# Fused matmul, GELU, matmul on one core: W1 sums of tiles 0 and 1 made in the head, sums of x(1) spread over four periods, W1 stores spread, the last output store issued by ScalarE

## The chip, the cores and the metric

One core of one Trainium2 chip. The metric is the device time of one execution in microseconds (us). The kernel before took 853.16 us in the median of six runs (853.0 to 853.53).

## The reference

```python
batch, m, k, h, n = 16, 512, 768, 3072, 768
def reference(x, w1, b1, w2):          # float32 in, float32 out
    y = np.matmul(x, w1) + b1
    y = 0.5 * y * (1.0 + erf(y / np.sqrt(2.0)))
    return np.matmul(y, w2).astype(np.float32)
```

## The kernel before

Both products are done with a seven-product scheme on 2x2 blocks: each output tile needs seven products of sums of blocks instead of eight products of blocks. The sums are made by VectorE in float16 (line L191, the helper `tt`). The 8192 rows are taken in eight groups of 1024; the argument is about the first two, x(0) and x(1), which share each W1 tile while it is in the on-chip memory. Cuts are marked with `# ...`.

W1 tile n arrives raw (four blocks); four sums complete it. The tile is later stored whole, to be read back for the other row groups:

```python
def keep(n):
    nc.sync.dma_start(out=w1s[hi_of(n)][:], in_=wts[n])

def prep_wt(n):
    o = {s: w1_op(wts[n], s) for s in range(7)}
    for d, a, b in ((T3, B22, T1), (T1, T1, B11), (T2, B22, T1), (T4, B21, T2)):
        later(KQ * P, lambda d=d, a=a, b=b: tt(o[d], o[a], o[b], SUB), soon)
```

TensorE works in periods. A period holds products p1, p5, p6, p2 of unit i and p7, p3, p4 of the unit before it, j; after each, `fill(slot)` puts other work into the queues:

```python
def copy_xy(u):                       # ScalarE; L604
    # ...
    nc.scalar.copy(out=bY[u.g % 2][:, 0:u.F], in_=bX[u.g % 2][:, 0:u.F])

def p7(u):
    u.mm(7, bY[u.g % 2], False, 0, u.C)
    add_c22(u)                        # VectorE; L611: reads bY
    # ...

def p6(u):
    u.mm(6, bY[u.g % 2], False, 0, u.C)
    # ... for the first row groups:
    nc.vector.tensor_copy(out=bZ[:, 0:u.F], in_=bY[u.g % 2][:, 0:u.F])   # L657

def period(i, j, fill):
    # ... (other kinds of units)
    p1(i, 0, i.C)
    copy_xy(i)
    p7(j)
    fill(1)
    p5(i)
    fill(2)
    p3(j)                             # VectorE add of bZ; L639
    fill(3)
    p6(i)
    j.right_done()                    # ScalarE GELU on what L611 and L639 made; L402
    fill(4)
    p4(j)                             # ScalarE GELU; L407
    fill(5)
    p2(i)                             # ScalarE GELU; L407
    fill(6)
```

Each engine takes its queue in order, so an instruction that waits holds up all behind it (in the timeline below VectorE stands 0.55 us at a load, and the add L639, which does not need it, comes after the sums that do). And p7 of a unit adds onto bY, so it can't start before L657 has read bY, while p6 needs bY filled by L604.

The first 24 periods are filled by `fill_a`. Period 7 is `at[1, 0]`, the first that uses x(1). The loads of the early phase are all issued at its start, W1 tile 6 last:

```python
def loads_a(pos):
    if pos == 0:
        load_wt(4)
        load_next_x(1, (0, 4, 1, 5))
        load_wt(5)
        load_next_x(1, (2, 6, 3, 7))
        load_wt(6)
    # ...

X1_PE = (3, 7)

def fill_a(pos, slot):
    # ...
    if pos == at[1, 0] - 2 and slot in (2, 5):
        transpose_pe(1, X1_PE[slot // 3])          # TensorE transposes, then a ScalarE copy
    if slot == (1 if pos < at[1, 0] else 4) and pos + 1 < len(seq) and seq[pos + 1][0] == 0:
        prep_wt(seq[pos + 1][1])                   # in period 5: W1 tile 6
    if slot == 4:
        if pos in (3, 6):
            prep_wt(pos // 6)                      # W1 tiles 0 and 1
        # ...
    if slot == 1:
        if pos in (at[1, 0] - 2, at[1, 0] - 1):
            h = pos - at[1, 0] + 2
            x_sums(1, soon, slice(h * RH // 2, (h + 1) * RH // 2))
        # ...
```

The last product of the last unit ends with two half sums, each stored at once:

```python
def last(self, banks):
    for t in range(2):
        self.mm(4, banks[t], True, 0, self.C, (t,))
        o = self.dst[:, 1, t, 0, :]
        tt(o, banks[t][:, t * N4:(t + 1) * N4], o, ADD)
        nc.sync.dma_start(out=orr[:, self.sb * 8 + 2 + t, N2:N2 + N4], in_=o)
```

Of the kernel before, what the change touches and what calls it, by code (L numbers as in the profile page):

```python
# [10 lines left out]
P = 128  # L11
ADD = mybir.AluOpType.add
SUB = mybir.AluOpType.subtract
# [4 lines left out]
B11, B21, T1, B22, T3, T2, T4 = range(7)  # L18
# [4 lines left out]
def kernel(  # L23
# [8 lines left out]
    nc = tc.nc  # L32
# [5 lines left out]
    RH = SB // 2  # L38
    nsb = R // SB
    KQ = K // P // 2  # L40
    NH = H // P // 2
    N2 = N // 2
# [3 lines left out]
    orr = out.rearrange("b (s p) n -> p (b s) n", p=P)  # L46
# [4 lines left out]
    N4 = N2 // 2  # L51
# [69 lines left out]
    def w1_op(wt, slot):  # L121
        raw = wt[:, 0:4 * KQ * P].rearrange("p (a k b c) -> p a b k c", a=2, k=KQ, b=2)
        if slot in RAW:
            return raw[:, RAW[slot][0], RAW[slot][1]]
        return wt[:, slot * KQ * P:(slot + 1) * KQ * P].rearrange("p (k c) -> p k c", c=P)
# [60 lines left out]
    with tc.manual_schedule():  # L186

        soon, queue, late, slow = [], [], [], []

        def tt(o, a, b, op):  # L190
            nc.vector.tensor_tensor(out=o, in0=a, in1=b, op=op)  # L191

        def later(n, f, q=None):
            (queue if q is None else q).append((70 + n * 0.52, f))

        def sums(ns):

            for q in (soon, queue):
                while q and ns >= q[0][0] * 0.6:
                    ns -= q[0][0]  # L200
                    q.pop(0)[1]()

        def flush(q):
            while q:
                q.pop(0)[1]()
# [18 lines left out]
        def keep(n):  # L224
            nc.sync.dma_start(out=w1s[hi_of(n)][:], in_=wts[n])

        def prep_wt(n):
            o = {s: w1_op(wts[n], s) for s in range(7)}
            for d, a, b in ((T3, B22, T1), (T1, T1, B11), (T2, B22, T1), (T4, B21, T2)):
                later(KQ * P, lambda d=d, a=a, b=b: tt(o[d], o[a], o[b], SUB), soon)  # L230

        def load_w2(k, c0, c1):
            nc.gpsimd.dma_start(out=w2rows[k][:, c0:c1, :], in_=w2r[:, k, c0:c1, :])
# [3 lines left out]
        def prep_w2(d, c, q):  # L237
            a, b = {T1: (T3, B11), T2: (B22, T1), T3: (B22, T3), T4: (B21, T2)}[d]
            o = [w2v[s][:, :, c:c + W2C, :] for s in (d, a, b)]
            later(2 * W2C * N4, lambda: tt(*o, SUB), q)  # L240
# [58 lines left out]
        def xT_of(sb, t):  # L299
            return XTs[sb][:, t // NU, :, (t % NU) * P:(t % NU + 1) * P]  # L300

        def transpose_dma(sb, t):
            nc.sync.dma_start_transpose(out=xT_of(sb, t), in_=xhs[t])
# [5 lines left out]
        def transpose_pe(sb, t, copy=nc.scalar.copy):  # L309
            for kc in range(2 * KQ):  # L310
                nc.tensor.transpose(out=bT[t % 2][:, kc, :], in_=xhs[t][:, kc * P:(kc + 1) * P],
                                    identity=ident[:])
            copy(out=xT_of(sb, t), in_=bT[t % 2][:])

        def blocks(sb):
            XT = XTs[sb]
            return [XT[:, a, c:c + KQ, :] for a in range(2) for c in (0, KQ)]

        def x_sums(sb, q, r=slice(0, RH), ks=range(4)):
            A11, A12, A21, A22 = [a[:, :, r] for a in blocks(sb)]  # L320
            S1, S2, S4 = [a[:, :, r] for a in XSs[sb]]
            n = KQ * len(range(RH)[r])
            ops = ((S1, A21, A22, ADD), (S2, S1, A11, SUB), (A21, A11, A21, SUB), (S4, A12, S2, SUB))
            for k in ks:
                later(n, lambda k=k: tt(*ops[k]), q)

        def g_sum(k, U, c0=0, c1=NH, q=None):
            G1, G2 = g_of(U // NU)
            r = slice(U % NU * P, (U % NU + 1) * P)
            g11, g21 = G1[:, c0:c1, 0, r], G1[:, c0:c1, 1, r]  # L330
            g12, g22 = G2[:, c0:c1, 0, r], G2[:, c0:c1, 1, r]
            s = [t[:, c0:c1, :] for t in GS]
            a, b, op = ((g21, g22, ADD), (s[0], g11, SUB), (g11, g21, SUB), (g12, s[1], SUB))[k]
            later((c1 - c0) * P, lambda: tt(s[k], a, b, op), q)
# [128 lines left out]
        class Unit3:  # L463
# [33 lines left out]
            def last(self, banks):  # L497
                for t in range(2):
                    self.mm(4, banks[t], True, 0, self.C, (t,))
                    o = self.dst[:, 1, t, 0, :]  # L500
                    tt(o, banks[t][:, t * N4:(t + 1) * N4], o, ADD)
                    nc.sync.dma_start(out=orr[:, self.sb * 8 + 2 + t, N2:N2 + N4], in_=o)

            def quarter(self, o, r, h):
                return o[:, r, :, h, :]
# [251 lines left out]
        def plain(n, row, side, half, r=slice(0, RH)):  # L757
            slot = ((B11, T1), (B21, B22))[half][side]
            for c in range(KQ):
                nc.tensor.matmul(out=banks[n, row][side][:, r], lhsT=w1_op(wts[n], slot)[:, c, :],  # L760
                                 rhs=blocks(0)[2 * row + half][:, c, r],
                                 start=half == 0 and c == 0 and r.start == 0,
                                 stop=half == 1 and c == KQ - 1, skip_group_check=True)

        def plain_done(n, row, side):
            nc.scalar.activation(out=Gs[0][side][:, n, row, :], in_=banks[n, row][side][:, 0:RH],
                                 func=GELU, bias=b1t[:, 2 * n + side:2 * n + side + 1])

        top, bottom = slice(0, 2 * P), slice(2 * P, RH)
        for half in range(2):  # L770
            for side in range(2):
                plain(0, 0, side, half)
        for side in range(2):
            plain_done(0, 0, side)
        plain(1, 0, 0, 0)
        transpose_pe(0, 4)
        plain(1, 0, 0, 1)
# [23 lines left out]
        plain_done(1, 1, 0)  # L801
        plain(1, 1, 1, 0, bottom)
        prep_wt(2)
        last = [soon.pop()]
        for k in (2, 3):
            for r in (top, bottom):
# [5 lines left out]
        seq = ([(0, k) for k in range(7)] +  # L812
               [(1, 0), (1, 1), (1, 2), (0, 7), (1, 3), (0, 8), (1, 4), (0, 9), (1, 6), (0, 10), (0, 11),
                (1, 5), (1, 10), (1, 11), (1, 7), (1, 8), (1, 9)])
        at = {u: n for n, u in enumerate(seq)}
# [21 lines left out]
                load_w2(*w2_at_pos[pos])  # L837

        X1_PE = (3, 7)

        def transposes_a(pos):
            for t in (pos - 1, pos + 3):
                if t not in X1_PE:
                    transpose_dma(1, t)

        def fill_a(pos, slot):
            if pos == 2 and slot == 1:
                plain(1, 1, 1, 1, bottom)
                plain_done(1, 1, 1)
            if pos == at[1, 0] - 2 and slot in (2, 5):  # L850
                transpose_pe(1, X1_PE[slot // 3])
            if slot == (1 if pos < at[1, 0] else 4) and pos + 1 < len(seq) and seq[pos + 1][0] == 0:
                prep_wt(seq[pos + 1][1])
            if slot == 4:
                if pos in (3, 6):
                    prep_wt(pos // 6)
                for m, c in ((21, 9), (22, 0), (23, 3), (23, 6)):
                    if pos == m:
                        prep_w2(T2, c, queue)
                        prep_w2(T3, c, late if m == 23 else queue)  # L860
                if pos == 23:
                    for c in range(0, NH, W2C):
                        prep_w2(T4, c, late)
            if slot == 1:
                if pos in (at[1, 0] - 2, at[1, 0] - 1):
                    h = pos - at[1, 0] + 2
                    x_sums(1, soon, slice(h * RH // 2, (h + 1) * RH // 2))
                if pos == at[0, NH - 1] + 2:
                    for c in range(0, NH, W2C):
                        prep_w2(T1, c, queue)  # L870
                    for k in (0, 1):
                        g_sum(k, 0)
            if pos > at[0, NH - 1]:
                if slot in (1, 4):
                    sums((0, 1100, 0, 0, 1500)[slot])
            elif slot in (1, 2, 4, 5):
                sums((0, 600, 300, 0, 600, 300)[slot])
            if slot == 5:
                loads_a(pos)
                if pos < 5:  # L880
                    transposes_a(pos)
                for n in {at[1, 0]: (0, 2, 3, 4, 6, 5), at[1, 1]: (1,)}.get(
                        pos, seq[pos][1:] if pos > at[1, 6] and seq[pos][0] and seq[pos][1] > 6 else ()):
                    keep(n)
            if slot == 6:
                flush(soon)
# [231 lines left out]
```

## Time and profile before

| | before |
|---|---|
| median of runs | 853.16 us |
| span of the profile | 851.49 us |
| TensorE busy | 844.9 us (99%) |
| VectorE busy | 667.0 us (78%) |
| ScalarE busy | 420.9 us (49%) |
| first useful matmul | 10.09 us |
| start of the last matmul | 847.62 us |
| TensorE gaps between 35 and 50 us, those over 0.06 us | 0.34 + 0.08 + 0.31 = 0.73 us |

A gap here is the time from one matmul's start to the next less the time in which the first streams its columns. I took that from matmuls that wait for nothing: 0.216 us for 512 columns in this trace. A gap is named by the start of the matmul before it: the gap at 41.1 us ends when TensorE goes on at 41.63 us. Gaps tell more than busy time does: the Trainium skill ("Trainium Kernel Development and Optimization", Performance Expectations) calls matmul busy time a bad metric for how close a kernel is to its roofline, because matmuls are pipelined.

The engine table and the chain of the page of the kernel before:

```profile
PE 844.9 (99%) x6432; PEld 568.8 (67%) x6432; DVE 667.0 (78%) x1128; ACT 420.9 (49%) x686; POOL 83.3 (10%) x135
...
PE 94%; DMA 4%; DVE 1%; ACT 0%; issue 0%; POOL 0%; DVEq 0%; ACTq 0%
```

TensorE (PE) is the bound; only its gaps can be saved. The timeline of the kernel before around the gaps (start in us, length in us, engine, line and operation, count, and in brackets the idle time before it and what ended it):

```profile
36.31 1.14 DVE L191 TENSOR_TENSOR arena<-arena 128x384 f16<-128x384 f16 x3 [0.55 <-DMA arena<-in_w_dram]
37.37 0.68 DVE L639 TENSOR_TENSOR arena<-bZ,arena 128x512 f32<-128x512 f32 x1
...
38.09 1.15 ACT L402 ACTIVATE arena<-arena,b1t 128x1024 f16<-128x1024 f32 x1 [0.91 <-DVE arena L639]
...
38.76 2.34 DVE L191 TENSOR_TENSOR arena<-arena 128x384 f16<-128x384 f16 x5
...
39.71 0.79 ACT L313 COPY arena<-bT 128x768 f16<-128x768 f16 x1
...
40.97 0.60 ACT L604 COPY bY<-bX 128x512 f32<-128x512 f32 x1
41.03 0.68 DVE L611 TENSOR_TENSOR arena<-bY,arena 128x512 f32<-128x512 f32 x1
...
41.63 1.46 PE L386 MATMUL bY<-arena 128*128 128x512 f16 x6 [0.17 <-ACT bY L604]
...
44.08 2.46 DVE L191 TENSOR_TENSOR arena<-arena 128x768 f16<-128x768 f16 x6
...
46.46 0.68 DVE L611 TENSOR_TENSOR arena<-bY,arena 128x512 f32<-128x512 f32 x1
```

Read from the top: ScalarE (ACT) has its activation L402. Behind that follows the second copy of transposed x (L313), and only then L604, for which TensorE waits at 41.6 us. Later six sums in a row push L611 to 46.46 us; that is the third gap.

The last stores, SyncE's (SP) queue in the timeline of the kernel before:

```profile
846.51 0.37 SPq L529 DMA_DIRECT2D out_dram<-arena  x1
...
847.50 0.37 SPq L523 DMA_DIRECT2D out_dram<-arena  x1
847.97 1.00 SPq L502 DMA_DIRECT2D out_dram<-arena  x2
```

The two stores of L502 start their issue 0.34 and 0.89 us after the start of the last matmul.

### The profile page before, as it was taken

What the parts mean: (1) busy time and instruction counts of PE and PEld (TensorE: products, weight loads), DVE (VectorE), ACT (ScalarE), POOL (GpSimd) and SP (SyncE); (2) the same over time, 40 slices, a digit from 0 to 9 for tenths busy, and PEclk for the clock granted to TensorE, in tenths of its full rate; (3) what the DMA queues carried; (4) which work ended last, traced back from release to release, by engine and by line L of the source; (5) the groups of instructions that cost most, each with busy time, mean ns of one, the idle gap of its engine ahead of it and who ended that gap; (6) DMA issues with size and microseconds to landing.
All of it is one profiled execution on the core that took longest, in us unless ns stands there. A gap on an engine that the chain in (4) does not pass through costs nothing.

```text
span 851.5 us, 16488 instructions
## 1 busy us (share of the span) xinstructions
PE 844.9 (99%) x6432; PEld 568.8 (67%) x6432; DVE 667.0 (78%) x1128; ACT 420.9 (49%) x686; POOL 83.3 (10%) x135
## 2 busy tenths in 40 slices
PE   8999999999999999999999999999999999999998
PEld 5444445687544897448974499645995469944798
DVE  4866678786657998579976799668996689956998
ACT  4777762122277512784138722477216771267611
POOL 5021100002100002000020000200002100010000
PEclk9999999999999999999999999999999999999999
DMA  9996986749999599987999689994999969984398
GB/s 227 213 256 89 253 169 244 267 184 221 212 340 226 186 326 372 304 183 233 334 368 292 141 283 335 360 294 113 312 335 355 277 128 325 347 322 172 100 298 295
DMA packets 143522, 219.05 MB, mean 257 GB/s; under 512 B 61756, under 2 KB 84724, under 8 KB 143444
## 3 DMA queue, kind: packets, MB, share of 16 engines
q1 hardware_dynamic: 117968, 179.83, 66.8%
q0 software_dynamic: 25440, 38.15, 20.7%
q8 instruction: 50, 0.82, 0.4%
q14 instruction: 28, 0.23, 0.1%
q10 hardware_dynamic: 36, 0.01, 0.0%
HBM read 180.30 MB, written 47.87 MB: 268 GB/s over the span
## 4 chain that ended last, share of the span: by engine, by line
PE 94%; DMA 4%; DVE 1%; ACT 0%; issue 0%; POOL 0%; DVEq 0%; ACTq 0%
PE bY L386 20%; PE bY L491 15%; PE bX L386 13%; PE bX L491 10%; PE bW L386 7%; PE bZ L386 7%; PE bZ L491 5%; PE bW L491 5%; PE bY L430 5%; DMA arena<-in_x_dram 3%; PE bZ L430 2%; PE bX L430 2%; PE bW L430 2%; DMA arena<-in_w_dram 1%; PE bY L578 1%; DVE arena L191 1%
## 5 line engine op out<-in xcount | busy, mean ns | idle before, releaser
L191 DVE TENSOR_TENSOR arena<-arena 128x1536 f16<-128x1536 f16 (+7 forms) x632 | 402.9, 668 | 7.8 <-DMA arena<-arena 1.6
L386 PEld LDWEIGHTS <-arena 128*128 128x128 f16 x1974 | 192.5, 98 | 224.7 <-issue 1.1
L491 PEld LDWEIGHTS <-arena 128*128 128x128 f16 x3528 | 292.1, 98 | 8.3 <-issue 0.4
L386 PE MATMUL bY<-arena 128*128 128x512 f16 x846 | 214.5, 379 | 0.3 <-ACT bY L604 0.2
L611 DVE TENSOR_TENSOR arena<-bY,arena 128x512 f32<-128x512 f32 (+1 forms) x102 | 69.3, 680 | 126.3 <-PE bY L386 87.6
L491 PE MATMUL bY<-arena 128*128 128x192 f16 x1500 | 138.3, 246 | 0.0
L386 PE MATMUL bX<-arena 128*128 128x512 f16 x564 | 138.2, 379 | 0.0
L604 ACT COPY bY<-bX 128x512 f32<-128x512 f32 (+1 forms) x143 | 78.6, 550 | 119.3 <-DVE arena L540 81.9
L402 ACT ACTIVATE arena<-arena,b1t 128x1024 f16<-128x1024 f32 x94 | 108.0, 1149 | 54.4 <-DVE arena L639 54.4
L624 ACT COPY arena<-bW 128x512 f32<-128x512 f32 (+1 forms) x147 | 81.0, 551 | 91.0 <-PE bW L491 43.9
L491 PE MATMUL bX<-arena 128*128 128x192 f16 x1020 | 93.1, 246 | 0.1
L639 DVE TENSOR_TENSOR arena<-bZ,arena 128x512 f32<-128x512 f32 (+1 forms) x102 | 69.2, 679 | 20.7 <-PE bZ L386 17.9
L386 PE MATMUL bZ<-arena 128*128 128x512 f16 x282 | 76.2, 379 | 0.0
L386 PE MATMUL bW<-arena 128*128 128x512 f16 x282 | 76.2, 379 | 0.0
L430 PEld LDWEIGHTS <-arena 128*128 128x128 f16 x528 | 51.6, 98 | 34.1 <-issue 0.2
L523 POOL DMA_DIRECT2D out_dram<-arena x42 | 30.5, 728 | 404.8 <-DVE arena L635 368.2
L407 ACT ACTIVATE arena<-bX,b1t 128x512 f16<-128x512 f32 x94 | 64.0, 681 | 10.0 <-PE bX L386 10.0
L407 ACT ACTIVATE arena<-bY,b1t 128x512 f16<-128x512 f32 x94 | 63.3, 673 | 0.0
L655 ACT COPY bZ<-bY 128x512 f32<-128x512 f32 (+1 forms) x54 | 29.0, 537 | 65.9 <-DVE arena L639 33.7
L297 POOL DMA_DIRECT2D arena<-in_x_dram x60 | 32.3, 544 | 250.8 <-DMA arena<-arena 141.3
L491 PE MATMUL bZ<-arena 128*128 128x192 f16 x504 | 48.5, 246 | 0.0
L491 PE MATMUL bW<-arena 128*128 128x192 f16 x504 | 48.5, 246 | 0.0
(60 smaller groups left out, 398.9 us busy)
## 6 DMA issues: line engine op xcount, KB each, us to landing
arena<-w2s SPq DMA_DIRECT2D x294, 288.0 KB, 4.6
arena<-w1s SPq DMA_DIRECT2D x72, 672.0 KB, 7.1
out_dram<-arena POOLq DMA_DIRECT2D x42, 384.0 KB, 7.2
w2s<-arena SPq DMA_DIRECT2D x49, 288.0 KB, 3.7
arena<-in_x_dram POOLq DMA_DIRECT2D x60, 192.0 KB, 7.3
w1s<-arena SPq DMA_DIRECT2D x12, 672.0 KB, 6.6
arena<-in_w_dram POOLq DMA_DIRECT2D x17, 384.0 KB, 7.4
out_dram<-arena SPq DMA_DIRECT2D x17, 384.0 KB, 3.3
```

The source lines that it names most:

```text
L191: nc.vector.tensor_tensor(out=o, in0=a, in1=b, op=op)
L297: nc.gpsimd.dma_start(out=xhs[t], in_=xr[:, sb * 8 + t, :])
L386: nc.tensor.matmul(out=dst[:, 0:RH], lhsT=w1_op(self.wt, slot)[:, c, :], rhs=a[:, c, :], start=first and c == 0, stop=c == self.C - 1, ski ...
L402: nc.scalar.activation(out=self.G[1][:, hi, :, :], in_=self.tmp, func=GELU, bias=b1t[:, 2 * hi + 1:2 * hi + 2])
L407: nc.scalar.activation(out=self.G[0][:, hi, row, :], in_=bank[:, 0:RH], func=GELU, bias=b1t[:, 2 * hi:2 * hi + 1])
L430: nc.tensor.matmul(out=dst[:, 0:N2], lhsT=a, rhs=w[:, :, c, :], start=first and c == 0, stop=c == self.C - 1, skip_group_check=True)
L491: nc.tensor.matmul(out=dst[:, t * N4:(t + 1) * N4], lhsT=a, rhs=w[:, c, :], start=first and c == 0 and t == ts[0], stop=c == NQ - 1, skip_ ...
L523: eng.dma_start(out=orr[:, s0:s0 + 2, right * N2:(right + 1) * N2], in_=self.dst[:, r].rearrange("p t h n -> p t (h n)"))
L604: nc.scalar.copy(out=bY[u.g % 2][:, 0:u.F], in_=bX[u.g % 2][:, 0:u.F])
L611: nc.vector.tensor_tensor(out=u.c22(), in0=bY[u.g % 2][:, 0:u.F], in1=w[:, 0:u.F], op=ADD)
L624: nc.scalar.copy(out=w[:, 0:u.F], in_=bW[:, 0:u.F])
L639: nc.vector.tensor_tensor(out=u.c12(), in0=bZ[:, 0:u.F], in1=w[:, 0:u.F], op=ADD)
```

## The change: intent and diff

Intent: take work out of VectorE's and ScalarE's queues where they are full (periods 5 to 7), so that TensorE no longer waits there, and save the issue time of one store at the end. Six of the eight sums of W1 tiles 0 and 1 go to the head, in an order that leaves raw block T1 alone until the plain products have used it. The sums of x(1) are queued in three periods instead of two, the last of them running into a fourth, and its second transpose on TensorE goes one period later. Five W1 stores go earlier.

```diff
-        def prep_wt(n):
+        def prep_wt(n, ks=()):
             o = {s: w1_op(wts[n], s) for s in range(7)}
-            for d, a, b in ((T3, B22, T1), (T1, T1, B11), (T2, B22, T1), (T4, B21, T2)):
-                later(KQ * P, lambda d=d, a=a, b=b: tt(o[d], o[a], o[b], SUB), soon)
+            early = ((T3, B22, T1, SUB), (T2, T3, B11, ADD), (T4, B21, T2, SUB), (T1, T1, B11, SUB))
+            usual = ((T3, B22, T1, SUB), (T1, T1, B11, SUB), (T2, B22, T1, SUB), (T4, B21, T2, SUB))
+            for d, a, b, op in [early[k] for k in ks] if ks else usual:
+                later(KQ * P, lambda d=d, a=a, b=b, op=op: tt(o[d], o[a], o[b], op), soon)
# ... last()
-                    nc.sync.dma_start(out=orr[:, self.sb * 8 + 2 + t, N2:N2 + N4], in_=o)
+                    (nc.sync, nc.scalar)[t].dma_start(out=orr[:, self.sb * 8 + 2 + t, N2:N2 + N4], in_=o)
# ... head
+        prep_wt(0, range(3))
+        flush(soon)
         for half in range(2):
             for side in range(2):
                 plain(0, 0, side, half)
         for side in range(2):
             plain_done(0, 0, side)
+        prep_wt(1, range(3))
+        flush(soon)
# ... fill_a
+        X1_AT = ((5, 2), (6, 1))
+        KEEP = {at[1, 0]: range(7), at[0, 7] + 1: (7,), at[0, 8]: (8,), at[0, 9]: (9,), at[0, 10]: (10,), at[0, 11]: (11,)}
# ...
-            if pos == at[1, 0] - 2 and slot in (2, 5):
-                transpose_pe(1, X1_PE[slot // 3])
+            if (pos, slot) in X1_AT:
+                transpose_pe(1, X1_PE[X1_AT.index((pos, slot))])
+            if pos == at[1, 0] - 1 and slot == 2:
+                x_sums(1, soon, slice(RH // 2, RH), (0, 1))
# ...
-                if pos in (3, 6):
-                    prep_wt(pos // 6)
+                if pos in (3, 4):
+                    prep_wt(pos - 3, (3,))
# ...
-                if pos in (at[1, 0] - 2, at[1, 0] - 1):
-                    h = pos - at[1, 0] + 2
-                    x_sums(1, soon, slice(h * RH // 2, (h + 1) * RH // 2))
+                if pos == at[1, 0] - 2:
+                    x_sums(1, soon, slice(0, RH // 2), (0, 1))
+                if pos == at[1, 0]:
+                    x_sums(1, soon, ks=(2, 3))
# ... W1 stores: for n in KEEP.get(pos, ()): keep(n)
#     before: six in period 7, one in period 8, five in periods 19 to 23
```

More of the change, by code (lines that the diff above doesn't have):

```diff
@@ L881, in fill_a @@
                     transposes_a(pos)
-                for n in {at[1, 0]: (0, 2, 3, 4, 6, 5), at[1, 1]: (1,)}.get(
-                        pos, seq[pos][1:] if pos > at[1, 6] and seq[pos][0] and seq[pos][1] > 6 else ()):
+                for n in KEEP.get(pos, ()):
                     keep(n)
```

## The prediction

> **What bounds the kernel now.** TensorE: the page has PE busy 844.9 of 851.5 us, and the chain that ended last is 94% PE. Matmuls that wait for nothing (128x512) start every 0.216 us in the timeline, so only PE's gaps can be saved. I summed the gaps between matmul starts beyond that. After the head (loads until 9.7 us), the early phase has three real ones: 0.34 us at 41.1 us (PE waits for ScalarE's copy of bX into bY, L604), 0.08 us at 45.95 (the same) and 0.31 us at 46.7 (waits for VectorE's add L611), together 0.73 us. Other gaps are thin (0.1 to 0.4 us per 10 us) and not touched.
>
> **Why.** In the timeline VectorE has a backlog there: 5 sums without a break (38.76 to 41.1) delay L611 to 41.03, and 6 (44.08 to 46.54) to 46.46. They hold the eight half sums of x(1) (128x768, 0.55 us each) and four of W1 tile 1 (128x384, 0.36 us). ScalarE is behind too: two copies of transposed x (0.80 us each) fell nearly into one period of 4.53 us, beside 3.7 us of regular work.
>
> **What the change does, costed.**
> - Six W1 sums (2.1 us of VectorE) move to the head, where VectorE idles 4.25 us before the copy at 14.9 us. Tile 0's can run from 10.7 us; PE reads tile 1 at 12.67 without a gap. Over by about 13.5 us: free.
> - The x(1) sums become 2, 2, then two whole ones (0.95 us each), in periods from about 33.5, 38.4 and 43 us; the W1 sums there go. By my walk through the queues L611 comes near 40.2 and 44.7 us (estimates).
> - The second PE transpose moves one period on: one ScalarE copy per period. L604 should end 0.4 us before PE needs it in the first period, only 0.1 us before in the next; a gap of up to 0.1 us may stay.
> - W1 stores: the same 12. Seven still go at about 38 us; five move from 86-94 to between 58 and 90 us, where the DMA share is 0.4 to 1.1 and PE has no gap. Worth nothing.
> - Last store: SyncE issues the last two at 847.97 and 848.51 us, 0.46 us each; ScalarE could issue the second at about 848.30. But DMA packets run nearly without a break until 850.16, at some 370 GB/s with 1536-byte packets. The Trainium skill ("DMA: Bandwidth & Descriptors", Issuing engines are not separate DMA queues) says that several issuers save only sequencer time, since the 16 DMA engines are shared; the trace agrees in that the drain lasts, not the issue. Worth 0.05 to 0.15 us.
>
> **Sum.** 0.6 to 0.73 us of gaps and 0.1 us of tail: 853.23 - 0.75 = 852.5 us, 0.09% less. Range 852.0 to 852.95. Faster by over 2%: 0.003; within: 0.992; slower: 0.005.
>
> **What would show it.** PE gaps at 41 and 46 us gone or under 0.1 us in sum; VectorE sums between 10.7 and 13.5 us; L611 following its PE group at once; output landing 0.1 us sooner after the last matmul.
>
> **What would make it wrong.** The last ScalarE copy still late (a new gap at 45.8 us); a whole 0.95 us sum pushing back L639 and so the activation; tile 1 landing late, holding VectorE and the copies of x; the ScalarE store saving 0.3 us, or starting slowly and losing some.

## The result, and the profile after

| | before | after |
|---|---|---|
| median of six runs | 853.16 us | 852.72 us (852.41 to 852.76) |
| ratio | | 0.9993, 95% interval 0.998 to 1.0006 |
| span of the profile | 851.49 us | 850.64 us |
| first useful matmul | 10.09 us | 9.52 us |
| first useful to last matmul (starts) | 837.54 us | 837.20 us |
| start of the last matmul to the end | 3.86 us | 3.92 us |
| TensorE gaps over 0.06 us between 35 and 50 us | 0.73 us | 0.25 us |

A ratio is the mean time of one kernel's fast runs over that of the other's of the same rounds, so it is not quite the ratio of the medians. The interval holds 1: the times alone don't prove the gain. In a second job (e9_after_again below) the ratio was 0.9995. Of the eleven runs of the changed kernel, ten were at or below 852.90 us, the lowest of all runs of the kernel before.

The spans differ by 0.85 us, and the table splits that: 0.57 us come from the first useful matmul, 0.34 from the stretch between first and last matmul, and 0.06 are lost at the end. Nothing of the change runs ahead of the first useful matmul (its first sum starts at 10.41 us); that start went from 9.27 to 10.30 us over the 14 profiles, in kernels of both kinds. So the 0.57 us are luck of the loads and not the change. Nor is 0.34 us the worth of the change: the experiments show that a quicker head lengthens the new gap described below, so some of the head's luck is taken back inside the stretch.

The engine table and the chain of the page after (lines of the code stand two lower: L386 is L388 here, L402 is L404, L604 is L606, L611 is L613, L639 is L641, L657 is L659):

```profile
PE 845.5 (99%) x6432; PEld 569.6 (67%) x6432; DVE 667.2 (78%) x1126; ACT 421.3 (50%) x686; POOL 84.1 (10%) x135
...
PE 95%; DMA 4%; DVE 0%; ACT 0%; issue 0%; POOL 0%; DVEq 0%; ACTq 0%
```

The timeline of the changed kernel in the same place:

```profile
36.14 1.14 DVE L191 TENSOR_TENSOR arena<-arena 128x384 f16<-128x384 f16 x3 [0.90 <-DMA arena<-in_w_dram]
37.20 0.68 DVE L641 TENSOR_TENSOR arena<-bZ,arena 128x512 f32<-128x512 f32 x1
37.20 1.46 PE L388 MATMUL bX<-arena 128*128 128x512 f16 x6
...
37.92 1.15 ACT L404 ACTIVATE arena<-arena,b1t 128x1024 f16<-128x1024 f32 x1 [1.48 <-DVE arena L641]
37.99 0.70 DVE L659 COPY bZ<-bY 128x512 f32<-128x512 f32 x1
...
38.74 0.81 PE L388 MATMUL bY<-arena 128*128 128x512 f16 x3
...
39.92 0.68 DVE L613 TENSOR_TENSOR arena<-bY,arena 128x512 f32<-128x512 f32 x1
40.11 0.59 ACT L606 COPY bY<-bX 128x512 f32<-128x512 f32 x1
...
41.01 1.46 PE L388 MATMUL bY<-arena 128*128 128x512 f16 x6
...
44.52 0.69 DVE L613 TENSOR_TENSOR arena<-bY,arena 128x512 f32<-128x512 f32 x1 [0.64 <-PE bY L388]
44.86 0.59 ACT L606 COPY bY<-bX 128x512 f32<-128x512 f32 x1
```

The old gaps are gone: L606 ends at 40.70 us, before TensorE needs it at 41.01, and at 45.45 before 45.55. L613 comes at 39.92 and 44.52 us (predicted 40.2 and 44.7). But there is a new gap. The six matmuls that start at 37.20 us stream until 38.49, and p7 starts at 38.74, 0.25 us later, when L659 is over (37.99 + 0.70 = 38.69). L659 is late because L641 is, and L641 because VectorE stood 0.90 us at the load of W1 tile 6.

VectorE in the head of the changed kernel (timeline):

```profile
10.41 1.14 DVE L191 TENSOR_TENSOR arena<-arena 128x384 f16<-128x384 f16 x3
11.74 1.14 DVE L191 TENSOR_TENSOR arena<-arena 128x384 f16<-128x384 f16 x3 [0.19 <-DMA arena<-in_w_dram]
14.39 0.56 DVE L315 COPY arena<-bT 128x768 f16<-128x768 f16 x1 [1.51 <-PE bT L313]
```

The six sums end at 12.9 us and delay nothing. The last stores of the changed kernel:

```profile
846.60 0.37 SPq L525 DMA_DIRECT2D out_dram<-arena  x1
847.06 0.44 SPq L504 DMA_DIRECT2D out_dram<-arena  x1
847.39 0.38 ACTq L504 DMA_DIRECT2D out_dram<-arena  x1
```

ScalarE starts the issue 0.67 us after the start of the last matmul, where SyncE did at 0.89 us. The last landing, however, comes 2.95 us after it in both kernels.

### The profile page after: what moved, and what is told of

It reads as the page before. It is cut to its first block, busy times and chain, and to the rows that moved or that the text cites. A ratio compares the mean times of both kernels' runs of the same rounds, so it can differ in the third digit from the quotient of the medians.

```text
span 850.6 us, 16487 instructions
## 1 busy us (share of the span) xinstructions
PE 845.5 (99%) x6432; PEld 569.6 (67%) x6432; DVE 667.2 (78%) x1126; ACT 421.3 (50%) x686; POOL 84.1 (10%) x135
## 4 chain that ended last, share of the span: by engine, by line
PE 95%; DMA 4%; DVE 0%; ACT 0%; issue 0%; POOL 0%; DVEq 0%; ACTq 0%
PE bY L388 21%; PE bY L493 15%; PE bX L388 14%; PE bX L493 10%; PE bZ L388 7%; PE bW L388 7%; PE bZ L493 5%; PE bW L493 5%; PE bY L432 5%; DMA arena<-in_x_dram 2%; PE bZ L432 2%; PE bW L432 2%; PE bX L432 2%; DMA arena<-in_w_dram 1%; PE bY L580 1%; PE bX L580 1%
## 5 line engine op out<-in xcount | busy, mean ns | idle before, releaser
L191 DVE TENSOR_TENSOR arena<-arena 128x768 f16<-128x768 f16 (+4 forms) x630 | 403.4, 671 | 7.5 <-PE bW L432 1.1
L388 PEld LDWEIGHTS <-arena 128*128 128x128 f16 x1974 | 192.6, 98 | 224.0 <-issue 0.4
L388 PE MATMUL bY<-arena 128*128 128x512 f16 x846 | 214.4, 379 | 0.1
L613 DVE TENSOR_TENSOR arena<-bY,arena 128x512 f32<-128x512 f32 (+1 forms) x102 | 69.4, 681 | 127.0 <-PE bY L388 90.3
L388 PE MATMUL bX<-arena 128*128 128x512 f16 x564 | 138.2, 379 | 0.0
L606 ACT COPY bY<-bX 128x512 f32<-128x512 f32 (+1 forms) x143 | 78.6, 550 | 119.4 <-DVE arena L542 82.0
L404 ACT ACTIVATE arena<-arena,b1t 128x1024 f16<-128x1024 f32 x94 | 108.0, 1149 | 54.0 <-DVE arena L641 54.0
L626 ACT COPY arena<-bW 128x512 f32<-128x512 f32 (+1 forms) x147 | 81.1, 552 | 90.7 <-PE bW L493 43.9
L641 DVE TENSOR_TENSOR arena<-bZ,arena 128x512 f32<-128x512 f32 (+1 forms) x102 | 69.3, 679 | 22.2 <-PE bZ L388 18.2
L388 PE MATMUL bW<-arena 128*128 128x512 f16 x282 | 76.2, 379 | 0.0
L388 PE MATMUL bZ<-arena 128*128 128x512 f16 x282 | 76.2, 379 | 0.0
L657 ACT COPY bZ<-bY 128x512 f32<-128x512 f32 (+1 forms) x54 | 29.0, 537 | 65.7 <-DVE arena L641 31.4
```

The lines of the kernel that those rows point to most:

```text
L191: nc.vector.tensor_tensor(out=o, in0=a, in1=b, op=op)
L388: nc.tensor.matmul(out=dst[:, 0:RH], lhsT=w1_op(self.wt, slot)[:, c, :], rhs=a[:, c, :], start=first and c == 0, stop=c == self.C - 1, ski ...
L404: nc.scalar.activation(out=self.G[1][:, hi, :, :], in_=self.tmp, func=GELU, bias=b1t[:, 2 * hi + 1:2 * hi + 2])
L613: nc.vector.tensor_tensor(out=u.c22(), in0=bY[u.g % 2][:, 0:u.F], in1=w[:, 0:u.F], op=ADD)
L626: nc.scalar.copy(out=w[:, 0:u.F], in_=bW[:, 0:u.F])
L641: nc.vector.tensor_tensor(out=u.c12(), in0=bZ[:, 0:u.F], in1=w[:, 0:u.F], op=ADD)
```

## The experiments

Twelve kernels ran, in three jobs. The theory at first was the prediction's, with one addition for the new gap. "Landing" below is the time at which W1 tile 6 had landed (its completion counts in the trace). "Gaps" are TensorE gaps over 0.06 us between 35 and 50 us.

| kernel | first useful | landing | last matmul | last less landing | gaps | released by |
|---|---|---|---|---|---|---|
| before | 10.09 | 36.28 | 847.62 | 811.34 | 0.34 + 0.08 + 0.31 | L604, L604, L611 |
| after | 9.52 | 36.11 | 846.72 | 810.61 | 0.25 | bY to bZ copy |
| e1 | 10.30 | 36.30 | 848.00 | 811.70 | none | |
| e2 | 9.27 | 36.05 | 846.60 | 810.55 | 0.07 + 0.08 | bY to bZ copy, bX to bY copy |
| e3 | 9.38 | 36.15 | 847.53 | 811.38 | 0.72 + 0.34 + 0.08 | bX to bY copy, bY to bZ copy, bX to bY copy |
| e4 | 9.61 | 36.09 | 846.89 | 810.80 | 0.13 + 0.09, at 48 to 50 us | bY to bZ copy, bX to bY copy |
| e5 | 9.71 | 36.65 | 847.34 | 810.69 | 0.43 + 0.08 | bY to bZ copy at 43.3 us |
| e6 | 10.26 | 36.37 | 847.18 | 810.81 | none | |
| e7 | 9.64 | 36.13 | 846.75 | 810.62 | 0.09 | bY to bZ copy |
| e8 | 9.53 | 36.31 | 846.90 | 810.59 | 0.42 | bY to bZ copy |
| e9 | 9.32 | 35.96 | 846.55 | 810.59 | 0.18 | bY to bZ copy |
| e10 | 9.72 | 37.30 | 847.92 | 810.62 | 1.15 | bY to bZ copy |
| e11 | 10.14 | 37.02 | 848.11 | 811.09 | 0.37 + 0.08 | bY to bZ copy at 43.8 us |
| e12 | 9.98 | 36.21 | 847.17 | 810.96 | none | |

### e1: the second transpose back

```diff
-        X1_AT = ((5, 2), (6, 1))
+        X1_AT = ((5, 2), (5, 5))
```

> The changed kernel with the second TensorE transpose of x(1) put back into the same period as the first (slot 5 of it). Theory (ScalarE's two 0.80 us copies in one period made the gap at 41.1 us; the new gap at 38.3 us exists because that transpose no longer fills TensorE while VectorE, held up by the load of W1 tile 6, finishes reading bY): the gap before p7 at 38.3 shrinks from 0.25 to under 0.1 us, and a gap of 0.3 to 0.7 us before the first p6 at about 41 us comes back, released by ScalarE's copy bX to bY. Rival (the VectorE backlog alone made the gap at 41): no gap over 0.1 us at 41. Sum of the early gaps (37 to 48 us) by theory 0.4 to 0.7 us, by rival under 0.15.

Measured: 853.14 us (four runs), ratio to before 0.9999. No gap between 35 and 50 us at all: what the rival expected at 41 us, and as the theory expected at 38. But the head was slow in this profile: first useful matmul at 10.30 us, and another gap of 0.77 us at 11.4 us, released by VectorE's cast of the last part of W1 tile 0, so TensorE was late against the loads by over a microsecond. VectorE then never waited for tile 6. So the run decides nothing alone, but it showed that these gaps depend on where TensorE stands against the landing of tile 6. e5 repeats the question without that wait.

### e2: the sums of W1 tile 6 later

```diff
-            if slot == (1 if pos < at[1, 0] else 4) and ...:
+            if slot == (1 if pos < at[1, 0] - 2 else 4) and ...:
                 prep_wt(seq[pos + 1][1])
# the half sums of x(1) of period 5 are queued in slot 4 behind them, not in slot 1
```

> The changed kernel with the four sums of W1 tile 6 queued three slots later (behind the bZ copy, when its load has landed), and the two half sums of x(1) of that period behind them. Theory (in-order VectorE stands 0.9 us at the load of tile 6, which delays the add of bZ and the copy bY to bZ, and TensorE's p7 waits for that copy): the VectorE wait for the in_w load is gone, the copy bY to bZ ends about 0.8 us sooner, the TensorE gap at 38.3 us (0.25) falls under 0.05, no other gap over 0.1 us between 37 and 48 us; stretch from first useful to last matmul 0.2 to 0.3 us shorter than the changed kernel's 837.20. Rival (TensorE reaches p7 too early for that copy in any case, since the transpose moved away): gap stays at 0.15 to 0.3 us.

Measured: 852.56 us (four runs), ratio 0.9991. The mechanism is as the theory has it. The timeline of e2:

```profile
36.08 0.69 DVE L641 TENSOR_TENSOR arena<-bZ,arena 128x512 f32<-128x512 f32 x1 [0.87 <-PE bZ L388]
...
36.87 0.70 DVE L659 COPY bZ<-bY 128x512 f32<-128x512 f32 x1
...
38.47 0.81 PE L388 MATMUL bY<-arena 128*128 128x512 f16 x3
```

VectorE now waits for TensorE (the last bracket) and not for the load, L659 ends at 37.57 instead of 38.69 us, and p7 starts without a gap. The stretch from first useful to last matmul, though, was 837.33 us, longer than the changed kernel's 837.20 and not 0.2 to 0.3 shorter: the first useful matmul was the earliest of all (9.27 us), and TensorE then waited 0.26 us at 12.3 us for a load of x. A quick head runs into the next load. The stretch was a bad measure for me to choose.

### e3: only the head sums, on the kernel before

The edit is `prep_wt` with its new orders, the two calls in the head and `prep_wt(pos - 3, (3,))`, on the kernel before.

> The kernel before with one part of the change: W1 sums of tiles 0 and 1 made in the head. Theory: the gap at 46.7 us (0.31, VectorE's add behind ten sums in a row) goes, since four sums leave that queue; the gap at 41.1 us (0.34, ScalarE) stays at 0.2 to 0.4 us. Rival (VectorE load in the periods before causes both): both gone.

Measured: 852.91 us (four runs), ratio 0.9994. The gap at 46.7 us went, as expected, and the one at 41 us stayed, larger (0.72 us) than I expected, because the head was quicker by 0.7 us than in the profile of before while tile 6 was not. A gap of 0.34 us before p7 at 43.9 us came in its place. From the landing to the last matmul it took 811.38 us, as in the kernel before (811.34). The head part alone gains nothing there.

### e4: only the x part, on the kernel before

The edit is `X1_AT` and the three lines with `x_sums(1, ...)`, on the kernel before.

> The kernel before with the other part: x(1) sums over four periods and the second transpose one period later; W1 sums of tiles 0 and 1 where they were. Theory: this part alone does all that the change does for TensorE: no gap over 0.1 us at 41 and at 46, the gap of 0.25 us at 38.3 as in the changed kernel (tile 6's sums still stand in front). Rival (the head part is needed): a gap over 0.15 us remains at about 46 us, where the sums of tile 1 still follow those of x(1).

Measured: 852.72 us (four runs), ratio 0.9992. No gap over 0.1 us at 41 or 46 us, as expected. The gap at 38.3 us was under 0.06 us, not 0.25. Two small ones stand at 48 to 50 us (0.13 and 0.09). Landing to last matmul took 810.80 us. So this part alone does most of the work, 0.54 us of it against the kernel before. The head part adds 0.19 us on top of it (810.80 against 810.61), each from one profile.

### e5: both transposes in one period, no wait for tile 6

e2's edit and e1's together.

> The kernel of e2_w1_tile6_later (no wait for tile 6 in front of the adds) with both TensorE transposes in one period, as in the kernel before. Theory now (the gap at 41.1 us in the kernel before comes from VectorE standing at the load of W1 tile 6, which lands at 36.1 to 36.3 us in every profile; the activation behind it and with it the copy bX to bY then come late, and the second transpose copy only adds to that): no gap over 0.1 us released by a ScalarE copy between 37 and 43 us. Rival (my prediction: two 0.80 us copies in one period are enough by themselves): a gap of 0.2 to 0.7 us at about 41 us, released by the copy bX to bY.

Measured: one look, 853.05 us against 853.30 in the same job. No gap released by a ScalarE copy between 37 and 43 us. The timeline of e5:

```profile
37.03 1.15 ACT L404 ACTIVATE arena<-arena,b1t 128x1024 f16<-128x1024 f32 x1 [0.39 <-DVE arena L641]
...
38.66 0.79 ACT L315 COPY arena<-bT 128x768 f16<-128x768 f16 x1
...
39.92 0.60 ACT L606 COPY bY<-bX 128x512 f32<-128x512 f32 x1
...
40.97 1.46 PE L388 MATMUL bY<-arena 128*128 128x512 f16 x6
41.98 0.56 DVE L191 TENSOR_TENSOR arena<-arena 128x768 f16<-128x768 f16 x1 [0.48 <-DMA arena<-arena]
```

The second transpose copy (L315) is there, and L606 still ends 0.45 us before TensorE needs it. In e3, with the wait, the activation L404 started at 37.95 us instead of 37.03, and L606 was late. In the changed kernel the activation is late (37.92) but the second copy is in the next period, and L606 is in time. So the gap at 41 us took both: the late add and the second copy. With both it is there (before, e3), with either alone it is not (the changed kernel and e4; e5 and e1). My prediction had only the second, beside a VectorE backlog. One reserve: e5 also queues the sums of x(1) later, so VectorE's queue is not the same there.

The last line shows what came instead: the sums of x(1) now wait for the DMA transposes of x(1), and a gap of 0.43 us opened at 43.3 us. e11 has the same (0.37 us). Moving the sums of tile 6 away from the wait moves the wait to the next piece that the loads bring.

### e10: the load of tile 6 delayed

```diff
                 load_next_x(1, (2, 6, 3, 7))
+                load_w2(0, 0, 1)
                 load_wt(6)
```

> The changed kernel with one further 0.39 MB load in front of W1 tile 6's on the same queue (the data is loaded again later, so results stay right). Theory (the early phase is anchored to the landing of tile 6): tile 6 lands about 1 us later than 36.1, VectorE's wait for it and the TensorE gap of 0.25 us before p7 at 38.3 grow by the same amount (gaps between 37 and 48 us add up to about 1.2 us, if the head is as quick as in the changed kernel's profile), and the time from landing to last matmul stays at 810.6 within 0.2. Rival (the gap has to do with the order on TensorE alone): gap stays at 0.25, last matmul moves by under 0.2 us.

Measured: one look, 853.63 us against 853.30 of before. Tile 6 landed at 37.30 us (1.19 later), the gap before p7 grew from 0.25 to 1.15 us, and from the landing to the last matmul it took 810.62 us. The list of waits of e10 between 34 and 48 us:

```profile
DVE arena L191 <- DMA arena<-in_w_dram: 1.8, 1, 1.8
...
PE bY L388 <- DVE bZ L659: 1.0, 1, 1.0
```

This settles the new gap. In the five profiles of the changed early phase in which the gap before p7 exists (after, e7, e8, e9, e10) the time from landing to last matmul is 810.59 to 810.62 us, while the landing moves by 1.34 us and the first useful matmul by 0.4. The early phase is anchored to the load: a quicker head only makes the gap longer. The measure holds only where TensorE comes early enough to wait. In e6 and e1 there is no early gap, and the time from the landing is 0.2 and 1.1 us longer because TensorE came later.

### e6 and e7: less to drain at the end

```diff
                 if u.ends:
-                    u.store(0)
+                    nc.sync.dma_start(out=orr[:, u.sb * 8, N2:N2 + 96], in_=u.dst[:, 0, 0, 0, 0:96])
```

The results are wrong (the rest of that block is not written). e7 has SyncE issue the last store as well.

> Wrong result on purpose: of the 384 KB store that is issued 0.12 us before the last matmul only 48 KB are sent, all else as in the changed kernel (last store by ScalarE). Theory (the end is limited by draining that store and the two after it, not by the issue of the last): last landing after the start of the last matmul falls from 2.95 to about 2.4 us. Rival (limited by the last store's issue and its own latency): stays at 2.85 to 2.95.

> As e6_short_store_act, but the last store issued by SyncE again. Theory (once the drain does not cover it, the issuer's 0.21 us counts): last landing about 2.6 us after the start of the last matmul, 0.15 to 0.25 later than with ScalarE. Rival (ScalarE's issue has a longer way to its first packet, which is why it gained nothing): no later than with ScalarE, within 0.05.

Measured, one look each: the last landing came 2.34 us (e6) and 2.29 us (e7) after the start of the last matmul, against 2.95. ScalarE's issue started at 0.67 us in e6 as in the changed kernel, so the last store's own issue did not make the 0.6 us. That holds against the rival of e6: the end is limited by what drains ahead of it. How much of the 0.6 us the missing bytes brought alone is not shown, because the store before the last was also issued 0.17 us sooner (at 0.17 instead of 0.34 us). For the issuer the pair is a miss. The short store needs a part of the result that is ready earlier, so SyncE issued it at 0.69 us before the last matmul instead of 0.12, had its queue free, and issued the last store at the same 0.67 us as ScalarE. At equal issue times ScalarE's store landed no sooner (0.05 us later).

### e8 and e9: W1 stores as before; the changed kernel again

e8 puts the old list of store positions back in place of `KEEP`; e9 is the changed kernel unedited.

> The changed kernel with the W1 stores at their old places. Theory (stores are off TensorE's path: no gap in 50 to 120 us in either kernel): same time as the changed kernel within 0.15 us in the median, gaps after 50 us within 0.1 us of 16.2 in sum. Rival (the stores in the early phase or at 86 to 94 us cost TensorE something): 0.2 us or more slower, with a gap over 0.1 us somewhere between 50 and 130 us.

> The changed kernel unedited, for more rounds and a second profile. Expected: 0.4 to 0.7 us below the kernel before. Theory (anchor): landing of tile 6 to the last matmul again 810.6 within 0.15 if the head is quick (first useful matmul before 9.8 us), with the gap before p7 at 38.3 us larger the quicker the head is; with a slow head no gap there and a longer stretch.

Measured, five runs each in one job: e8 852.59 us, e9 852.76 us, before 853.25 us (nine runs). e9's runs went from 852.25 to 853.53; its ratio is 0.9995 (0.9983 to 1.0008), e8's 0.9992 (0.998 to 1.0005). Gaps after 50 us add up to 16.23 and 16.22 us. (This count, like the 16.2 of the expectation, takes less streaming time for a matmul than the 0.216 us above and so holds much of the pipeline's own time; only the difference counts.) Landing to last matmul took 810.59 us in both. The W1 stores' places are worth nothing. e9's gain of 0.49 us in the medians is inside what was expected; but its gap before p7 (0.18 us) was smaller than the first profile's (0.25) though the head was quicker, since tile 6 landed 0.15 us sooner too and TensorE lost 0.12 us at 10.4 us. My expectation there had left the landing's own scatter out.

### e11 and e12: both waits attacked, with either issuer

e2's edit, and at the end one big store of a sum 1.8 us earlier and the store of the last product's top half in two parts:

```diff
                     for r in range(2):
                         later(2 * N2, lambda r=r: tt(par[1][:, r], par[1][:, r], par[3][:, r], ADD), soon)
+                        if self.sb + 1 == nsb and r == 0:
+                            later(2 * N2, lambda: self.c22_sum(0), soon)
# ... left_done
+                if row == 0 and self.ends:
+                    self.store_quarter(0, 0)
# ... p3
-                    u.store(0)
+                    u.store_quarter(0, 1)
# ... fill_mm2_two
-                if sb + 1 == nsb and slot in (1, 2):
-                    units3[5].c22_sum(slot - 1)
+                if sb + 1 == nsb and slot == 2:
+                    units3[5].c22_sum(1)
```

> The changed kernel with tile 6's sums later (as in e2) and the last stores spread: one of the two big stores before the end goes 1.8 us sooner, when the DMA engines are idle, and the store of the last product's top half goes in two parts, the left as soon as it is there; ScalarE issues the last. Theory (drain-limited end): last landing 2.4 to 2.6 us after the start of the last matmul instead of 2.95. With tile 6: 0.5 to 0.8 us below the changed kernel at best, 0.3 at worst where the loads of x hold the head. Rival (fixed latency after the last sum): landing stays at 2.85 to 2.95, gain over the changed kernel under 0.25 us.

> As e11_both with the last store issued by SyncE. Theory (with the drain out of the way the issuer counts): last landing 0.1 to 0.25 us later than in e11_both, but 0.06 us of that given back at the end, where the waits run in another order: span from last matmul to the end 0.05 to 0.2 us longer than in e11_both. Rival (ScalarE's issue never helps): equal or shorter.

Measured, five runs each in the job of e8 and e9: e11 853.62 us, e12 853.44 us, ratios to before 1.0004 and 1.0005. Both miss: the last landing came 3.12 and 3.09 us after the start of the last matmul instead of 2.4 to 2.6, a new TensorE gap of 0.30 us opened 3.3 us before the start of the last matmul, and e11 needed 1.33 us from the last landing to the end instead of 0.97. Three things went wrong, as the trace shows. The sum moved forward delays VectorE's later work by 0.3 us, which is the gap. The store that I moved was not in the way: in the kernel before, the DMA engines were busy only two thirds of the time between 844.0 and 844.8 us, behind that store's packets and ahead of the rest, so what drains after them was the same 1.9 MB. And the top half's store in two parts goes in packets of 768 bytes instead of 1536. In the kernel before these moved about 325 and 370 GB/s, so 0.39 MB takes 1.21 instead of 1.06 us (an estimate from these rates), 0.15 us more, and the landing came 0.14 and 0.17 us later. A side effect stands in SyncE's queue, in the timeline of e11:

```profile
840.76 0.40 SPq L525 DMA_DIRECT2D out_dram<-arena  x1
841.25 1.27 SPq L288 DMA_DIRECT2D arena<-w2s  x1
```

The earlier store waits for its sum and holds up the last load of W2 behind it, which SyncE issued at 838.0 us in the kernel before. So the theory that the drain limits the end was not refuted, but my edit made the drain longer. The issuer again made no gain: in e12 SyncE issued the last store 0.26 us later than ScalarE in e11 (0.93 against 0.67 us), and its landing came 0.03 us sooner.

No experiment gave a version that clearly beats the changed kernel (e2 with 852.56 and e8 with 852.59 us are within the scatter of its 852.72 and 852.76). The changed kernel with the last store back on SyncE, which by the numbers below should be some 0.07 us quicker (an estimate from seven and three profiles), was not run.

### What the profiles say together about the last store

| last store by | profiles | issue starts | last landing | end |
|---|---|---|---|---|
| SyncE | before, e3, e4 | 0.88 to 0.89 | 2.94 to 2.95 | 3.85 to 3.86 |
| ScalarE | after, e1, e2, e5, e8, e9, e10 | 0.67 | 2.95 to 2.96 | 3.91 to 3.94 |

Times are us after the start of the last matmul. The means of the end are 3.857 and 3.924 us: in the kernels in which ScalarE issues the last store the end comes 0.067 us later. The Trainium skill ("DMA: Bandwidth & Descriptors", Issuing engines are not separate DMA queues) says that it only saves the sequencer's time; the trace agrees, with 0.21 us of issue saved and nothing of the landing. Where the loss comes from is seen in the trace: at the end of the program SyncE waits for the stores' counts one after another, about 0.06 us for each. In the kernel before the wait for the last landing (850.58 us) is the last one. In the changed kernel another follows (849.69, then 849.75 us), and in e11 seven follow. Seven follow in e12 too, where SyncE issues the last store, and none in e6, where ScalarE does. So by these traces it counts where the last landing stands in the list of waits; which engine issues the store matters only as far as it changes that.

## Why the prediction was right or wrong

The time was right: 852.72 us lies in the range of 852.0 to 852.95, and the class "within 2%" is right. The saving was 0.44 us in the medians, where I had predicted about 0.75. Of the 0.31 us between them the last store explains 0.17 (0.1 gained by prediction, 0.067 lost by measurement); the other 0.14 stays open. Point by point:

- **"The bound is TensorE; the early gaps of 0.73 us can be saved": right.** All three gaps are gone in both profiles of the changed kernel, and from the landing of tile 6 to the last matmul it takes 0.73 us less (811.34 to 810.61). That both numbers are 0.73 is luck: the second also holds a gap at 508 us (below) and the different pace of the two heads.
- **"0.6 to 0.73 us of gaps" as the net: right in size, but the mechanism lacked a wait.** In the pair of profiles the gaps fell by only 0.73 - 0.25 = 0.48 us, which looks like a miss. But TensorE came earlier to the load there: from the first useful matmul to the landing it took 26.19 us before and 26.59 after. In e6, whose edit touches only the end, it took 26.11 us, nearly as before. e6 (one profile) has no early gap, and its stretch from first useful to last matmul is 836.92 us, 0.62 less than in the kernel before. So the predicted saving was there. What I left out stood in the first line of the profile shown above: VectorE waiting for W1 tile 6, 0.55 us in the kernel before. This load sets the pace in the changed kernel wherever the head is quick: a gap of 0.25 us in the first profile after, 0.18 in e9, 0.42 in e8, 1.15 in e10 where the load was delayed. These gaps take back a quick head's lead.
- **"ScalarE is behind: two copies of transposed x": half right.** e5 has both copies in one period and no gap at 41 us. It takes the late add behind the wait for tile 6 as well. This is the step of the mechanism that failed: I took the copies for the whole cause. That the change cured the gap nonetheless is partly luck, since taking away either of the two causes was enough.
- **Head sums "over by about 13.5 us: free": right** (12.9 us). Alone they gain nothing (e3). The x part alone brings 0.54 us from landing to last matmul (e4); the head sums then add 0.19.
- **L606 "only 0.1 us before in the next" period: right** (45.45 us against 45.55), with no gap.
- **W1 stores "worth nothing": right** (e8).
- **Last store "worth 0.05 to 0.15 us": wrong in sign.** The reasoning that the drain decides was right, and e6 agrees. From that zero should have followed, so this is the term of the sum that was mis-sized. It cost 0.067 us, through one more wait at the program's end.

What stays open: 0.62 us less (e6) to 0.73 us less (from the landing) up to the last matmul and 0.067 us more at the end should make some 0.55 to 0.66 us; the medians differ by 0.44 and 0.49 us. The runs scatter by 0.3 to 1.3 us, with landing times of tile 6 that differ from profile to profile (35.96 to 36.37 us in kernels whose loads were alike, 36.65 and 37.02 in e5 and e11, for which I have no cause), so I can't tell whether the rest is chance. One gap at 508 us is about 0.09 us longer in every profile that has the x part than in before and e3 (0.16 to 0.18 against 0.07 to 0.09); why, I did not look into. And a single gap of 0.25 us, at 387 us before and 386 us after, is left in both kernels. It ends with the same kind of copy (L604, L606 after), and nobody attacked it.

The cost of a sum fits a page as well. The Trainium skill ("VectorE: DVE Perf Modes", the section on SBUF-source ops that pay a fixed extra latency per instruction) gives (N + 151)/0.96 ns for a float32 sum, and its table of perf modes puts 16-bit sums at twice the rate. With N halved for float16, an estimate from that page is 357, 557 and 957 ns for 384, 768 and 1536 columns; the traces have 0.36, 0.55 to 0.56 and 0.95 us. So the two sums of x(1) that the change makes whole cost 0.95 us each instead of two times 0.55, which saves about 0.3 us of VectorE in total.

## What to carry to other kernels

When several waits stand one behind the other, find the earliest one that is tied to something outside the engines, a load for instance, and measure from its end: times from there repeated within 0.03 us in the five profiles where TensorE waited for it, while the last matmul's time from the program's start moved by 1.37 us (by 0.35 us without e10, whose load was delayed on purpose). An engine that comes to the anchor earlier, by a quicker head or because work was moved behind the anchor (here one transpose, 0.33 us of TensorE), gains nothing by it: the lead comes back as a new gap in front of the anchor. The sum of gaps of two profiles with different heads then says too little of what was saved; compare profiles in which the head kept the same pace. An earlier issue of the last store was worth nothing here while the stores ahead of it were still draining; look at when the last packet ends before moving an issue.

## What the Trainium skill lacked or had wrong

- No page that I read has the cost of the waits at the end of a program: SyncE waits for each outstanding store in turn, about 0.06 us apart, and if the store that lands last is not the last in that order, the rest is added behind it (0.067 us in the changed kernel; in e11 1.33 us instead of 0.97 us from last landing to the end, in e12 1.35).
- "DMA: Bandwidth & Descriptors" (Issuing engines are not separate DMA queues) says that issuing from several engines saves the sequencer's time. It lacks that this can be a loss: 0.21 us of issue saved, landing unchanged, end 0.067 us later.
- The same page (Anatomy of one DMA) says, for DMAs issued by GpSimd, that most of the fixed 2 us is the receipt of the write in the target memory. For a store issued by SyncE to idle DMA engines the trace of the kernel before has 0.91 us from the start of the issue (842.24 us) to its first packet (843.15), and at the end of the program 0.35 us from the end of the last packet to the last landing. The first-byte latency that the page's table of specifications gives for the sync and scalar path, about 0.6 us, is less than these 0.91 us. For such a store I found no figure there for the time from the last packet to the landing.
